# A two-layer backbone kernel: a new order for the end of the first projection

## The chip, the cores and the metric

The kernel runs on one core of one Trainium2 chip, as a single program. The metric is the device time of one execution in microseconds (us). The core has five engines that run side by side, each through its own instructions in order: TensorE (PE in the profile; its weight loads are PEld), VectorE (DVE), ScalarE (ACT), GpSimd (POOL), and SyncE (SP), which here only issues transfers. Transfers (DMA) are issued from SyncE's or ScalarE's queue, and an issue that has to wait holds up everything behind it on that queue.

## The reference, cut to what matters

Two layers run over 1024 latent tokens and 256 context tokens, 1024 features wide. The change lies in the first layer, windowed attention with 16 query heads in 4 groups, one key and value head per group:

```python
q, k, v, g = jnp.split(h @ w_in, [A_WIDTH, A_WIDTH + A_KV_WIDTH, A_WIDTH + 2 * A_KV_WIDTH], axis=-1)
...
qx = apply_rope(qx, cos, sin)
kx = apply_rope(kx, cos, sin)
...
yx = (ox * jax.nn.silu(gx)) @ w_out
```

`h` is the normalized input, scaled and shifted by a vector that comes from the conditioning (adaLN). `w_in` is 1024 x 2560: columns 0 to 1023 are queries, 1024 to 1279 keys, 1280 to 1535 values, 1536 to 2559 gates. A query block of 128 latent tokens sees its own and the two neighbouring blocks of keys under a band mask, and all context keys; a context block sees the context only. Rope turns queries and keys of latent tokens, not of context tokens. Layer two (latent attention) follows on the result.

## The kernel before, in words

**Arithmetic.** Products that matter are done as three: each factor is split in a rounded high part (a cast on ScalarE, L121) and a low part (a subtraction, L122, on VectorE or GpSimd), and `mm3` (L126 to L128) adds high x high, low x high and high x low.

**First projection.** `w_in` is taken in ten blocks of 256 columns, in the order of the list `blocks`; the first is the values' and is done by tokens. For the other nine, `proj_t(bi, gp, c)` computes one tile: block `bi`, token group `gp` (0: the 256 context tokens; 1 and 2: 512 latent tokens each), half `c` of the block's columns. A latent tile has 24 matmuls of 512 columns; a context tile does both halves, 48 matmuls of 256 columns. I write a tile as (bi, gp, c). What follows the matmuls depends on the columns:

- gates (c0 at 1536 or above): Silu on ScalarE into a buffer (L462), then a store to DRAM from SyncE's queue (L465, L467);
- queries and keys of latent tokens: rope, that is a product and a shuffle on VectorE (L489, L490), a product and, for queries, a sum on GpSimd (L491, L493); then, after the next tile's matmuls are written, `rest()`: the split (ScalarE, VectorE), and one tile later the store of the queries (L510);
- queries of context tokens: split and store only (L478, L483).

Weights come by `fetch(bi)`: four loads into three staging buffers, split on ScalarE and GpSimd within the two tiles after the request. There are two weight places, used in turn. The list `order` says which tile follows which; `next_item()` counts tiles and runs what `later` has put off. All of this stands inside a manual schedule, in which each engine's instructions keep the order in which the code writes them; behind it (from L802) the compiler's scheduler may reorder.

**Beside the tiles**, `ada_steps` computes the remaining adaLN vectors on VectorE (L385) from pieces of `ada_w`, summed by two or one small matmuls (L396), some of them stored as gate vectors (L408).

**The end of the projection.** In before the last two blocks are gates (columns 2048 and 2304), and their tiles are interleaved by token group: (8,1,*), (9,1,*), (8,2,*), (9,2,*), (8,0,0), (9,0,0). In that stretch the kernel also requests and splits the output weights `a_w_out` (16 pieces of 128 x 512, L691, through three staging buffers `wstg`, by `wo_load`, the lower part in turn on GpSimd and VectorE) and prepares the attention. A unit is 128 query tokens times one group of four heads (`UnitA`). `prep_q` loads its queries (four transfers, L566), `prep` its gates (L574), `score(h)` multiplies queries with keys for one head (L590, L591, two or four matmuls), takes the maxima under the mask (L597, VectorE, with L599) and the exponents (L600, ScalarE). `T` transposes them (L618), `PV` multiplies with the values (L628), `fin` and `fin2` finish a unit. In before unit 0's four scores stand whole in front of tile (9,0,0). A tile of the psum memory (`PB`, eight banks) is given out in turn: `pss()` for the projection, banks 0 to 2 for scores.

The memory of gates and tables is shared by offset: the mask lies where the cosines lay, the gate vectors `gx` where the sines and, after the change, a staging buffer lie.

Of the kernel before, what the change touches and what calls it, by code (L numbers as in the profile page):

```python
# [59 lines left out]
def kernel(ctx: ExitStack, tc: tile.TileContext, t, out, dbg=None):  # L60
    nc = tc.nc
# [21 lines left out]
    load = nc.sync.dma_start  # L83
# [35 lines left out]
    def split(hi, lo, src, lo_eng=None):  # L119

        nc.scalar.copy(hi, src)  # L121
        (lo_eng or nc.vector).tensor_sub(lo, src, hi.bitcast(F32))  # L122

    def mm3(o, a, b, first, last):
        (ah, al), (bh, bl) = a, b
        nc.tensor.matmul(o, ah, bh, start=first, stop=False)  # L126
        nc.tensor.matmul(o, al, bh, start=False, stop=False)  # L127
        nc.tensor.matmul(o, ah, bl, start=False, stop=last)  # L128
# [135 lines left out]
        return t["x"][(i - 2) * 128 : (i - 1) * 128, :]  # L264

    w_in = t["a_w_in"]
    blocks = [1280, 0, 1536, 256, 1792, 512, 768, 1024, 2048, 2304]
    wt = {}


# [171 lines left out]
        hw.append(two.rearrange("p (q s k n) -> p q s k n", q=2, s=2, k=8))  # L442
    swap = [(i + 16) % 32 for i in range(32)]

    def proj_t(bi, gp, c):
        W, c0 = wt[bi], blocks[bi]
        ps = PB[:, 4, :] if (bi, gp) == (9, 0) else pss()
        for cc in (c,) if gp else range(2):
            if gp:
                o = shp(ps, 2, 256)  # L450
            else:
                o = ps[:, cc * 256 : cc * 256 + 256]
            for k in range(8):
                if gp:
                    m = [hw[gp][:, :, s, k, :] for s in range(2)]
                else:
                    m = [hT[0][:, s, k, :] for s in range(2)]
                mm3(o, [W[:, s, k, cc * 128 : cc * 128 + 128] for s in range(2)], m, k == 0, k == 7)
        t0 = 256 + 512 * (gp - 1) if gp else 0
        if c0 >= 1536:  # L460
            g = ev.next()
            nc.scalar.activation(g, ps, AF.Silu)  # L462
            ch = (c0 - 1536) // 128
            if gp:
                load(out=g0_d[ch + c, :, t0 : t0 + 512], in_=g)  # L465
            else:
                load(out=g0_d[ch : ch + 2, :, 0:256].rearrange("c p n -> p c n"), in_=shp(g, 2, 256))  # L467
            return None
        if gp == 0:
            if c0 == 1024:  # L470
                u = shp(ps, 2, 256)
                for e in range(2):
                    kh = kT[:, e::2, 0:256]
                    split(kh[0:64], kh[64:128], u[64 * e : 64 * e + 64])
            else:
                q = shp(qst.next(), 2, 2, 2, 128)
                u = shp(ps, 2, 2, 128)
                split(q[:, :, :, 0].bitcast(F32R), q[:, :, :, 1].bitcast(F32R), u)  # L478

                def store():  # L480
                    for cc in range(2):
                        dst = q0_d[c0 // 256, cc, :, :, 0:2].rearrange("e p t s n -> (e p) (t s n)")
                        load(out=dst, in_=q[:, cc].rearrange("p t s n -> p (t s n)"))  # L483

                later(1, store)
            return None
        x0 = t0 - 256
        a, r = ev.next(), ev.next()
        nc.vector.tensor_mul(a, ps, cosa[:, x0 : x0 + 512])  # L489
        nc.vector.stream_shuffle(out=r, in_=ps, mask=swap)  # L490
        nc.gpsimd.tensor_mul(r, r, sina[:, x0 : x0 + 512])  # L491
        if c0 < 1024:
            nc.gpsimd.tensor_add(a, a, r)  # L493
# [23 lines left out]
    gx = f_at(8, 1024)  # L517
    gc = f_at(48, 1024)
    ytmp = Ring(F, [12], 512)
    wstg = Ring(F, [4, 6, 12], 512)  # L520
    rbr = Ring(F, [42, 47], 256)
    or1, or2, rtr = (Ring(F, [o, o - 5], 256) for o in (43, 44, 45))
    Pr = Ring(F, [14 + 2.5 * i for i in range(8)], 640)
# [156 lines left out]
    units = [UnitA(ti, g) for ti in ORDER for g in range(4)]  # L680


    def wo_load():
        engs = [nc.gpsimd, nc.vector]
        pieces = [(k, slice(c * 512, c * 512 + 512)) for k in range(8) for c in range(2)]
        staged = []
        for i in range(len(pieces) + 2):
            if i < len(pieces):
                k, cs = pieces[i]
                st = wstg.next()  # L690
                load(out=st, in_=t["a_w_out"][k * 128 : k * 128 + 128, cs])  # L691
                staged.append((k, cs, st))
            if i >= 2:
                k, cs, st = staged.pop(0)
                split(Wo[k][:, 0, cs], Wo[k][:, 1, cs], st, engs[i % 2])
                yield

    wo_fill = wo_load()
    order = [(bi, gp, c) for bi in range(1, 8) for gp in range(3) for c in range(2 if gp else 1)]
    order += [(bi, gp, c) for gp in (1, 2, 0) for bi in (8, 9) for c in range(2 if gp else 1)]  # L700
    rest = None


# [65 lines left out]

    in_order = tc.manual_schedule()  # L770
    in_order.__enter__()
    for bi, gp, c in order:
        next_item()
        if bi + 1 < 10 and bi + 1 not in started:
            started.add(bi + 1)
            fetch(bi + 1)
        steps(ada_steps, 1 if gp and blocks[bi] < 1536 else 2)
        if (bi, gp, c) == (9, 2, 0):
            load2(out=mask, in_=t["mask"])
            load2(out=gx, in_=gate_d[0, 0, :].partition_broadcast(128))  # L780
            load2(out=gc, in_=gate_d[0, 1, :].partition_broadcast(128))
        if (bi, gp) == (8, 0):
            units[0].prep_q()
            units[0].prep()
            units[1].prep_q()
        if (bi, gp) == (9, 0):
            units[1].prep()
            units[2].prep_q()
            for h in range(4):
                units[0].score(h)  # L790
        r = proj_t(bi, gp, c)
        if rest:
            rest()
        rest = r
        if bi >= 8 and gp != 1:
            for _ in range(2):
                next(wo_fill, None)

    while due:
        next_item()  # L800
# [13 lines left out]
    og = None  # L814
    fins = []
    for ui, u in enumerate(units):
        if ui in (1, 2):
            next(wo_fill, None)
            next(wo_fill, None)
        if u.g == 0:  # L820
            og = shp(ogr.next(), 2, 8, 128)
            steps = 4 * u.m - 2
# [737 lines left out]
```

## Time and profile before

| what | value |
|---|---|
| median of 3 runs | 1650.68 us (1650.03 to 1650.99) |
| the profiled execution | 1647.58 us |
| its span, first to last instruction | 1645.8 us |
| mean granted TensorE clock | 0.994 |
| TensorE busy | 1588.9 us, 97% of the span |
| ScalarE, VectorE, GpSimd busy | 825.8, 991.7, 801.4 us |

How to read it: the profile is of one execution; each row is an instruction or a group with its line in the code, `out<-in` by the program's names, and in brackets the idle time before it with what ended it. A `q` behind an engine's name (SPq, ACTq) is its queue, issuing a transfer. The granted clock is the share of full speed that TensorE had. Matmuls are pipelined, so a row's length is more than the distance to the next one, and it is the distance that counts.

### The profile page before, as it was taken

Reading aid. Unit: us, or ns where it says so; the run is one execution under the profiler, and the core shown is the slowest. Engines: PE = TensorE matmul, PEld = TensorE weight load, DVE = VectorE, ACT = ScalarE, POOL = GpSimd, SP = SyncE. Lnnn points to the kernel's source line nnn. Section 1 sums busy time; section 2 is a strip of 40 time slices with the busy share of each in tenths; the row PEclk is TensorE's granted clock in tenths of the full one; section 3 lists DMA queues with packets and bytes.
Section 4 is the critical chain, followed back from the end, with each engine's and each line's share of the span. In section 5 each row is a group of like instructions: output and inputs, shape, how many; then the busy total and the mean of one; then the engine's idle time right before and its main releaser. Section 6 shows DMA issues by size and latency. Waiting matters only on the chain.

```text
span 1645.8 us, 23776 instructions
## 1 busy us (share of the span) xinstructions
PE 1588.9 (97%) x8156; PEld 1211.1 (74%) x8156; DVE 991.7 (60%) x1972; ACT 825.8 (50%) x1779; POOL 801.4 (49%) x776
## 2 busy tenths in 40 slices
PE   7899999988999999998999999999999999999998
PEld 2687888776878888878887887566766756666687
DVE  1786878648888888878444005655455455455354
ACT  3622121249777777777323324555555555555421
POOL 1453456214543333344245422786676777668510
PEclk9999999999999999999999999999999999999999
DMA  8535445374333222235127722211111111122151
GB/s 279 158 116 192 165 162 173 117 220 138 98 107 93 92 90 90 91 109 176 52 78 249 231 67 87 77 52 36 39 39 36 45 37 38 46 80 70 47 160 64
DMA packets 122467, 176.75 MB, mean 107 GB/s; under 512 B 11485, under 2 KB 71517, under 8 KB 122345
## 3 DMA queue, kind: packets, MB, share of 16 engines
q1 hardware_dynamic: 120184, 171.12, 32.7%
q10 hardware_dynamic: 2160, 4.11, 0.8%
q8 instruction: 64, 1.05, 0.3%
q14 instruction: 59, 0.48, 0.1%
HBM read 129.04 MB, written 46.15 MB: 106 GB/s over the span
## 4 chain that ended last, share of the span: by engine, by line
PE 75%; DVE 8%; ACT 6%; issue 5%; POOL 3%; DMA 2%; SPq 0%; ACTq 0%; DVEq 0%; POOLq 0%
PE PB L126 17%; PE PB L128 16%; PE PB L127 16%; PE PB L1233 9%; PE PB L1199 4%; PE PB L628 3%; PE PB L618 3%; DVE arena_r L122 2%; PE PB L590 2%; PE PB L591 1%; DVE arena_f L597 1%; ACT arena_r L121 1%; ACT arena_f L600 1%; DVE arena_f L202 1%; ACT arena_f L1218 1%
## 5 line engine op out<-in xcount | busy, mean ns | idle before, releaser
L126 PE MATMUL PB<-arena_r 128*128 128x512 f32 (+3 forms) x1632 | 605.6, 372 | 6.3 <-ACT arena_r L205 3.8
L127 PE MATMUL PB<-arena_r 128*128 128x512 f32 (+3 forms) x1632 | 597.4, 366 | 5.1 <-DVE arena_r L207 3.9
L128 PE MATMUL PB<-arena_r 128*128 128x512 f32 (+3 forms) x1632 | 594.5, 366 | 0.2 <-DVE arena_r L122 0.2
L126 PEld LDWEIGHTS PB<-arena_r 128*128 128x128 f32 (+1 forms) x1632 | 309.2, 190 | 96.3 <-issue 32.0
L1225 POOL TENSOR_TENSOR arena_f<-arena_f 128x512 f32<-128x512 f32 x252 | 327.5, 1299 | 75.4 <-ACT arena_f L1218 60.1
L128 PEld LDWEIGHTS PB<-arena_r 128*128 128x128 f32 (+1 forms) x1632 | 309.2, 190 | 49.9 <-issue 1.2
L127 PEld LDWEIGHTS PB<-arena_r 128*128 128x128 f32 (+1 forms) x1632 | 310.4, 190 | 47.8 <-DVE arena_r L207 5.1
L1203 DVE TENSOR_REDUCE arena_f<-PB 128x1 f32<-128x1280 f32 x128 | 190.4, 1488 | 104.9 <-PE PB L1199 102.4
L1218 ACT ACTIVATE arena_f<-PB 128x512 f32<-128x512 f32 x320 | 189.1, 598 | 124.7 <-PE PB L128 111.8
L122 DVE TENSOR_TENSOR arena_r<-PB,arena_r 128x512 fp32r<-128x512 f32 (+4 forms) x255 | 162.5, 644 | 120.7 <-ACT arena_r L121 118.8
L122 POOL TENSOR_TENSOR arena_r<-arena_f,arena_r 128x512 fp32r<-128x512 f32 x84 | 116.7, 1402 | 192.3 <-ACT arena_r L121 165.2
L121 ACT CAST arena_r<-PB 128x512 fp32r<-128x512 f32 (+4 forms) x255 | 138.2, 549 | 67.6 <-PE PB L618 30.7
L597 DVE CUSTOM_DVE_ANT_0 arena_f<-PB,arena_f,small 128x256 f32<-128x256 f32 (+1 forms) x288 | 145.5, 522 | 26.9 <-PE PB L591 20.2
L1233 PE MATMUL PB<-arena_f 128*64 128x512 f32 x640 | 157.1, 600 | 0.0
L600 ACT ACTIVATE arena_f<-arena_f,small 128x640 f32<-128x640 f32 (+2 forms) x160 | 119.3, 746 | 32.7 <-DVE small L599 32.2
L628 PE MATMUL PB<-arena_r 128*128 128x512 f32 x336 | 123.5, 441 | 4.0 <-ACT arena_f L639 2.5
L385 DVE SCALAR_TENSOR_TENSOR arena_f<-arena_f,small 128x512 f32<-128x512 f32 x98 | 114.1, 1208 | 11.4 <-DMA arena_f<-ada_w 11.0
L618 PE MATMUL PB<-ident,arena_f 128*128 128x128 f32 x672 | 111.3, 274 | 2.2 <-ACT arena_f L600 1.2
L121 ACT CAST arena_r<-arena_f 128x512 fp32r<-128x512 f32 (+1 forms) x124 | 72.9, 608 | 75.8 <-DMA arena_f<-a_w_in 21.2
L1233 PEld LDWEIGHTS PB<-arena_f 128*64 128x64 f32 x640 | 43.5, 136 | 80.9 <-issue 79.4
L1199 PE MATMUL PB<-arena_r 96*128 96x512 f32 (+1 forms) x384 | 99.8, 367 | 0.3 <-DVE arena_f L1203 0.2
L618 PEld LDWEIGHTS PB<-ident,arena_f 128*128 128x128 f32 x672 | 83.5, 140 | 20.9 <-ACT arena_f L600 5.4
(151 smaller groups left out, 1788.8 us busy)
## 6 DMA issues: line engine op xcount, KB each, us to landing
arena_r<-q_d SPq DMA_DIRECT2D x160, 128.0 KB, 2.9
arena_f<-ada_w SPq DMA_DIRECT2D x68, 256.0 KB, 3.1
arena_f<-a_w_in SPq DMA_DIRECT2D x40, 256.0 KB, 3.7
arena_f<-x SPq DMA_DIRECT2D x16, 512.0 KB, 3.9
q_d<-arena_f SPq DMA_DIRECT2D x16, 512.0 KB, 2.6
qn_d<-arena_f SPq DMA_DIRECT2D x16, 512.0 KB, 4.5
arena_r<-qn_d SPq DMA_DIRECT2D x32, 256.0 KB, 3.6
arena_f<-ada_w SPq DMA_DIRECT2D x14, 512.0 KB, 6.0
```

Source lines behind the costliest of these rows:

```text
L121: nc.scalar.copy(hi, src)
L122: (lo_eng or nc.vector).tensor_sub(lo, src, hi.bitcast(F32))
L126: nc.tensor.matmul(o, ah, bh, start=first, stop=False)
L127: nc.tensor.matmul(o, al, bh, start=False, stop=False)
L128: nc.tensor.matmul(o, ah, bl, start=False, stop=last)
L618: nc.tensor.transpose(pt[:, h, :], self.Ps[h][:, ci * 128 : ci * 128 + 128], ident)
L628: nc.tensor.matmul(self.pv, V[:, self.chunks[ci], self.g, :], PT[:, s], start=ci == 0 and s == 0, stop=ci == self.m - 1 and s == 1,)
L1199: nc.tensor.matmul(psm[:, n0 : n0 + n], self.qT[0:96, 0, b * 128 : b * 128 + 128], kt[0:96, 0, n0 : n0 + n], start=True, stop=True,)
L1203: nc.vector.reduce_max(self.mx[:, 96 + b : 97 + b], psm[:, 0:TOK], AX.X, negate=True)
L1218: nc.scalar.activation(E, S, AF.Exp)
L1225: eng.tensor_add(self.acc, self.acc, E)
L1233: nc.tensor.matmul(self.pv[p : p + 64], Vq[:, c, self.h % 4, :], self.E.pop(c), start=c < 2, stop=c >= NT - 2)
```

## The change

Six edits, all around the end of the first projection:

1. `blocks`: the order of the last blocks becomes gates 2048, keys 1024, gates 2304, queries 768 (it was queries 768, keys 1024, gates 2048, gates 2304).
2. `order`: the last two blocks run (8,1,*), (8,2,*), (9,1,*), (9,2,*), then (8,0,0) and (9,0,0).
3. Gate stores go out on ScalarE's queue (`load2`) instead of SyncE's (`load`).
4. Output weights: `wo_get(3)` requests three pieces after each of the last five tiles, `wo_cut(3)` splits three before that after each of the last four (GpSimd, VectorE, GpSimd); the rest follows at units 0 and 1 on GpSimd. The third staging buffer moves from 12 to 8.
5. `proj_t` takes a list of functions and runs one after every fourth step of its inner loop, so unit 0's four scores stand inside tile (9,0,0), behind its 6th, 18th, 30th and 42nd matmul.
6. The mask is loaded at tile (8,0,0) instead of (9,2,0), the gate vectors `gx` and `gc` at unit 2 instead of (9,2,0).

```diff
-    blocks = [1280, 0, 1536, 256, 1792, 512, 768, 1024, 2048, 2304]
+    blocks = [1280, 0, 1536, 256, 1792, 512, 2048, 1024, 2304, 768]
...
-    def proj_t(bi, gp, c):
+    def proj_t(bi, gp, c, between=()):
+        between = iter(between)
...
                 mm3(o, [W[:, s, k, cc * 128 : cc * 128 + 128] for s in range(2)], m, k == 0, k == 7)
+                if k % 4 == 1:
+                    for fn in [next(between, None)]:
+                        fn and fn()
...
-                load(out=g0_d[ch + c, :, t0 : t0 + 512], in_=g)
+                load2(out=g0_d[ch + c, :, t0 : t0 + 512], in_=g)
             else:
-                load(out=g0_d[ch : ch + 2, :, 0:256].rearrange("c p n -> p c n"), in_=shp(g, 2, 256))
+                load2(out=g0_d[ch : ch + 2, :, 0:256].rearrange("c p n -> p c n"), in_=shp(g, 2, 256))
...
-    wstg = Ring(F, [4, 6, 12], 512)
+    wstg = Ring(F, [4, 6, 8], 512)
...
+    def wo_get(n):
+        for _ in range(min(n, len(wo_pieces))):
+            k, cs = wo_pieces.pop(0)
+            wo_got.append((k, cs, wstg.next()))
+            load(out=wo_got[-1][2], in_=t["a_w_out"][k * 128 : k * 128 + 128, cs])
+
+    def wo_cut(n, engs):
+        for i in range(min(n, len(wo_got))):
+            k, cs, st = wo_got.pop(0)
+            split(Wo[k][:, 0, cs], Wo[k][:, 1, cs], st, engs[i % len(engs)])
...
-    order += [(bi, gp, c) for gp in (1, 2, 0) for bi in (8, 9) for c in range(2 if gp else 1)]
+    order += [(bi, gp, c) for bi in (8, 9) for gp in (1, 2) for c in range(2)] + [(8, 0, 0), (9, 0, 0)]
+    tail = len(order) - 5
...
-        steps(ada_steps, 1 if gp and blocks[bi] < 1536 else 2)
-        if (bi, gp, c) == (9, 2, 0):
-            load2(out=mask, in_=t["mask"])
-            load2(out=gx, in_=gate_d[0, 0, :].partition_broadcast(128))
-            load2(out=gc, in_=gate_d[0, 1, :].partition_broadcast(128))
         if (bi, gp) == (8, 0):
             units[0].prep_q()
+            load2(out=mask, in_=t["mask"])
             units[0].prep()
             units[1].prep_q()
         if (bi, gp) == (9, 0):
             units[1].prep()
             units[2].prep_q()
-            for h in range(4):
-                units[0].score(h)
-        r = proj_t(bi, gp, c)
+            first = [lambda h=h: units[0].score(h) for h in range(4)]
+        steps(ada_steps, 1 if gp and blocks[bi] < 1536 else 2)
+        r = proj_t(bi, gp, c, first if (bi, gp) == (9, 0) else ())
         if rest:
             rest()
         rest = r
-        if bi >= 8 and gp != 1:
-            for _ in range(2):
-                next(wo_fill, None)
+        if at > tail:
+            wo_cut(3, [nc.gpsimd, nc.vector, nc.gpsimd])
+        if at >= tail:
+            wo_get(3)
...
-        if ui in (1, 2):
-            next(wo_fill, None)
-            next(wo_fill, None)
+        if ui < 2:
+            wo_cut(3, [nc.gpsimd])
+            wo_get(3)
+        if ui == 2:
+            load2(out=gx, in_=gate_d[0, 0, :].partition_broadcast(128))
+            load2(out=gc, in_=gate_d[0, 1, :].partition_broadcast(128))
```

More of the change, by code (lines that the diff above doesn't have):

```diff
@@ L680 @@
     units = [UnitA(ti, g) for ti in ORDER for g in range(4)]
[L683 to L698, printed above, removed]
+    wo_pieces = [(k, slice(c * 512, c * 512 + 512)) for k in range(8) for c in range(2)]
+    wo_got = []
+    def wo_get(n):
[7 more added lines that the diff above has]
+            split(Wo[k][:, 0, cs], Wo[k][:, 1, cs], st, engs[i % len(engs)])
     order = [(bi, gp, c) for bi in range(1, 8) for gp in range(3) for c in range(2 if gp else 1)]
-    order += [(bi, gp, c) for gp in (1, 2, 0) for bi in (8, 9) for c in range(2 if gp else 1)]
+    order += [(bi, gp, c) for bi in (8, 9) for gp in (1, 2) for c in range(2)] + [(8, 0, 0), (9, 0, 0)]
+    tail = len(order) - 5
     rest = None
@@ L771 @@
     in_order.__enter__()
-    for bi, gp, c in order:
+    for at, (bi, gp, c) in enumerate(order):
         next_item()
```

## The prediction

> **What bounds the kernel now.** I read the page's first line, then the surroundings of the change in the table of stretches (us from the span's start; length; busy time and instructions of PE, PEld, DVE, ACT, POOL; granted clock; DMA share; GB/s).
>
> ```profile
> span 1645.8 us, 23776 instructions
> ```
>
> ```profile
> 300.00:346.50 46.50, 43.68 (x184) 33.17 (x183) 22.31 (x26) 11.74 (x20) 9.86 (x8) 1.00 0.57 183
> 346.50:365.60 19.10, 16.55 (x114) 15.28 (x113) 7.58 (x26) 8.10 (x16) 2.56 (x2) 0.91 0.73 203
> 357.00:361.00 4.00, 3.91 (x18) 3.56 (x18) 3.02 (x16) 2.77 (x7) 0.00 (x0) 0.57 0.91 266
> 365.60:400.00 34.40, 30.57 (x190) 24.52 (x189) 30.91 (x115) 32.98 (x82) 13.94 (x18) 1.00 0.49 142
> ```
>
> TensorE is the bound: up to 346.5 it is busy for all but 2.8 us, so only its holes can be won. Then it does the two context tiles (8,0,0) and (9,0,0) until 365.6 and, between them, four scores; after 365.6 ScalarE is busy for 32.98 of 34.40 us and is the engine to watch. The holes, from TensorE's timeline:
>
> ```profile
> 312.59 0.51 PE L126 MATMUL PB<-arena_r 128*128 128x512 f32 x1 [0.33 <-ACT arena_r L121]
> 313.93 0.50 PE L127 MATMUL PB<-arena_r 128*128 128x512 f32 x1 [0.84 <-POOL arena_r L122]
> ...
> 339.93 0.59 PE L396 MATMUL PB<-arena_f,small 128*1 128x512 f32 x1 [1.60 <-DVE arena_f L385]
> ...
> 346.27 0.39 PE L128 MATMUL PB<-arena_r 128*128 128x512 f32 x1
> 346.49 0.28 PE L126 MATMUL PB<-arena_r 128*128 128x256 f32 x1
> ...
> 352.13 0.28 PE L128 MATMUL PB<-arena_r 128*128 128x256 f32 x1
> 354.54 0.36 PE L590 MATMUL PB<-arena_r 128*128 128x256 f32 x1 [2.14 <-DMA arena_r<-q_d]
> ...
> 365.49 0.28 PE L590 MATMUL PB<-arena_r 128*128 128x256 f32 x1
> ```
>
> Three holes: 1.17 us at 312-314 (last quarter of block 9's weights), 1.60 us at 339.9 (an adaLN sum), and the scores. From 346.49 to 352.13 lie 48 matmuls of (8,0,0), one per 0.12 us; a 512-wide one takes 0.22 (346.27 to 346.49). The scores' first matmul waits for the queries' load until 354.54. From 352.25 to 365.49, 13.2 us, TensorE does 16 score matmuls and the 48 of (9,0,0), worth 64 x 0.12 = 7.7: 5.5 us are lost there. 1.7 of them are the clock: 0.57 over 357-361 means 0.43 / 0.5 x 4 = 3.4 us at half speed. SyncE's queue, and what it waited for from 300 to 420, tell why the queries are late:
>
> ```profile
> SPq L465 <- ACT arena_f L462: 23.7, 6, 4.9
> SPq L691 <- POOL arena_r L122: 10.0, 5, 3.7
> ```
>
> ```profile
> 347.78 2.19 SPq L691 DMA_DIRECT2D arena_f<-a_w_out  x2
> 350.02 0.28 SPq L408 DMA_DIRECT2D gate_d<-arena_f  x1
> 350.40 0.69 SPq L566 DMA_DIRECT2D arena_r<-q_d  x1
> ```
>
> SyncE stood behind gate stores and output-weight loads. Unit 0's queries are asked for at 350.40 and used 4.14 us later.
>
> **The change, part by part** (times on the clock of before).
>
> *Gate stores to ScalarE's queue.* SyncE loses waits of 23.7 us; ScalarE gains an issue per store. Cost 0 before 365: ScalarE is busy for 11.74 of 46.5 and 8.10 of 19.1 us. Were that cover gone, each would cost the 0.34 to 0.48 of its present issues (rows below).
> The Trainium skill, page "DMA: Bandwidth & Descriptors", section "Issuing engines are not separate DMA queues", speaks against it: another issuing engine saves only the issue time, as all share 16 DMA engines. The trace differs in that the wait, not the issue, held SyncE; by page or row the sum gets 0, for no hole of TensorE names a gate store.
>
> *Order of the last blocks.* Block 9's weights, asked for at block 8's start, are now first used four tiles later instead of two: the 1.17 us goes. The adaLN sum's products no longer sit behind output-weight requests, and one more gate block ahead of block 8 moves them earlier: the 1.60 us goes. Sum -2.8, so the last 512-wide tile, (9,2,1), ends at 343.7 instead of 346.5. Bounds -2 (a new short wait) and -3.3.
>
> *Queries as last block.* This is the expensive part: rope now runs on GpSimd in the very tiles in which it should cut output weights. In before the last ten tiles are all gates, and GpSimd is idle there. A query tile of before, VectorE, then GpSimd, then a cut among rope work:
>
> ```profile
> 226.40 0.69 DVE L489 TENSOR_TENSOR arena_f<-PB,arena_f 128x512 f32<-128x512 f32 x1 [1.76 <-PE PB L128]
> ```
>
> ```profile
> 225.75 1.29 POOL L122 TENSOR_TENSOR arena_r<-arena_f,arena_r 128x512 fp32r<-128x512 f32 x1
> 227.83 1.64 POOL L491 TENSOR_TENSOR arena_f<-arena_f 128x512 f32<-128x512 f32 x1 [0.79 <-DVE arena_f L490]
> 229.55 1.62 POOL L493 TENSOR_TENSOR arena_f<-arena_f 128x512 f32<-128x512 f32 x1
> ...
> 244.73 1.55 POOL L122 TENSOR_TENSOR arena_r<-arena_f,arena_r 128x512 fp32r<-128x512 f32 x1 [2.68 <-ACT arena_r L121]
> ```
>
> GpSimd's rope ends 229.55 + 1.62 - 226.40 = 4.8 us after the tile's psum is read, about 4.9 after the tile's end; a cut costs it 1.29 (up to 1.55).
>
> *Output weights a tile early.* Sixteen pieces pass three buffers, three per tile; two of three are cut on GpSimd, each cut stands behind the rope of its own tile, and the next three requests wait on SyncE for the cuts. Durations of loads of the weights, then of the queries, to landing:
>
> ```profile
> DMA to landing us min/median/max: 2.6/3.0/3.4
> ```
>
> ```profile
> DMA to landing us min/median/max: 2.6/2.9/5.0
> ```
>
> The chain: (9,2,0) ends at 343.7 - 24 x 0.225 = 338.3, its rope at 343.2; two cuts of the first three pieces, 345.8; rope of (9,2,1), ready 0.15 + 1.43 after 343.7, starts at 345.8, ends at 349.1; the second three, last one requested at 345.9 and landed at 348.9, cut on GpSimd until 349.1 + 2 x 1.29 = 351.7. Only then does SyncE issue the last of the third three (0.4), a query store (0.4), and from 352.5 unit 0's queries: first score at 352.5 + 4.14 = **356.7**. It is the early request itself that delays the queries: they stand behind it on SyncE, and with them unit 1's queries and gates, not needed until 365.
>
> *First scores inside the last tile.* TensorE ends (8,0,0) at 343.7 + 5.76 = 349.5, does six matmuls of (9,0,0) and stands at the first score from 350.2 to 356.7: 6.5 us with 42 matmuls of the tile behind it. Then 16 + 42 = 58 x 0.12 = 7.0 us, plus half clock. I take the stretch seen, 1.7 us lost (bounds 0, as until 357, and 3.4, two such stretches). VectorE's maxima and the exponents go beside the tile, so their pace no longer counts. End: **365.4**, against 365.49: -0.1.
> The Trainium skill, "TensorE: Matmul & The Clock Gate", section "What's actually happening", gives half speed after an idle window of about 3.4 us and full speed after about 3.4 us busy. Before shows it already after a 2.1 us hole with sparse scores behind; by the page a hole of 6.5 us has it too, so the end is 365.4 by either.
> The mask's load, now behind the second cuts on ScalarE's queue (349.4), may take up to 7 us before it is the later one; its landing isn't shown.
>
> *Behind the tile*, ScalarE:
>
> ```profile
> L121 ACT CAST arena_r<-arena_f 128x512 fp32r<-128x512 f32 x6 | 3.5, 622 | 0.0
> ...
> L462 ACT ACT_TABLE_LOAD x1 | 1.3, 1283 | 4.4 <-PE PB L128 4.4
> L600 ACT ACT_TABLE_LOAD x1 | 1.3, 1283 | 0.0
> ...
> L462 ACT ACTIVATE arena_f<-PB 128x512 f32<-128x512 f32 x1 | 0.6, 598 | 0.0
> ```
>
> ```profile
> 337.31 0.48 ACTq L780 DMA_DIRECT2D arena_f<-gate_d  x1
> ...
> 360.43 0.72 ACT L600 ACTIVATE arena_f<-arena_f,small 128x512 f32<-128x512 f32 x1 [0.41 <-DVE small L599]
> 361.06 0.19 ACT L600 ACTIVATION_READ_ACCUMULATOR arena_f<-arena_f,small 128x1 f32 x1
> ```
>
> Gone behind 365.6: two table loads and a Silu, 3.2 us. New there: the last head's exponent, 0.9; the query cast, 0.6; a seventh weight cast, 0.6; two gate-vector issues at unit 2, 1.0: 3.1 us. Sum -0.1; as to order, bounds -2 and +1. VectorE is even (one cut and a query subtraction for three cuts).
>
> Sum: -0.1 - 0.1 = -0.2, and the profiled span 1645.6. The median of the runs before, 1650.68, lies 3.1 above the profiled execution's 1647.58, so the difference is carried over: **1650.5 us**. With the bounds of its terms this case runs from 1647.5 to 1654.
>
> **The rivals.**
> *Faster: the queries arrive in time.* If GpSimd cut the weights ahead of its rope, SyncE would reach the queries before 346, and only the mask would make TensorE wait, about 1 us. End: 349.5 + 7.7 + 1 = 358.2, 7.3 earlier: 1643.4 us. For it: SyncE loses 23.7 us of waits. Against: POOL's rows run one after another in the order written, and 244.73 shows cuts behind rope. Chance 0.18.
> *Slower: the same wait, longer.* Place: the first score inside (9,0,0). Each us by which the queries land after 356.7 is a us of the kernel; a landing of 5.0 for 2.9 (+2.1), four cuts at 1.55 (+1.0), and a second stretch at half clock (+1.7) give +4.8: 1655.5 us. It decides from a first score after 360.0. For it: everything up to that score is one chain without slack. Against: 5.0 is the longest landing seen. Chance 0.22.
> The same page says that the gate's window runs freely, which by itself allows that second stretch; no run here shows its phase.
> *Slightly faster: ScalarE's relief carries on.* The table loads go at once, the gate vectors and seventh cast come later, perhaps into slack: -2.5, 1648.2. For it: ScalarE is idle for only 1.4 of 34.4 us after 365.6. Against: unit 0's last exponent now lies there too. Chance 0.14.
> That the change does not do what it says is the forecast: its holes close and one opens.
>
> **How the numbers follow.** Forecast 0.46. About 0.2% (3.3 us) is what a measurement of this kernel can tell from no change. Faster by more: 0.18 and a third of the last rival, 0.23. Slower by more: 0.22. Within: 0.55. The range 1644.5 to 1655.5 leaves out most of the faster rival and a little of the slower one, and holds the bounds of the forecast's terms.
>
> **What would show it.** Right: no hole at 312 or at the adaLN sum; cuts on GpSimd straight behind rope; SyncE asking for unit 0's queries about 8.8 us after (9,2,1) ends; a hole of 5 to 8 us at the first score, inside (9,0,0), released by the queries' load; clock under 1 behind it; units' scores at about the same time as now. Wrong: the first score without a wait (the faster rival), a hole at another line, or a different end with the same hole.

## The result, and the profile after

| | before | after |
|---|---|---|
| median of 12 runs | 1649.97 us | 1651.15 us |
| lowest and highest | 1645.31, 1651.34 | 1649.69, 1652.85 |
| profiled execution, its span | 1647.58, 1645.8 | 1652.48, 1650.3 |
| mean granted clock | 0.994 | 0.990 |

The ratio is 1.0013, with a 95% interval of 1.0004 to 1.0022: 2.1 us slower (0.7 to 3.6; a ratio's distance from 1, times 1650); the two medians lie 1.2 us apart. I had forecast 0.2 us faster. That the median of 1651.15 lies only 0.65 above the 1650.5 of the forecast is in part luck: its baseline, 1650.68 from three runs, is 1649.97 with twelve.

In the diff's region all line numbers are 4 higher after the change: L594 and L595 are the scores, L570 the queries' loads, L694 the output weights' loads, L514 the queries' stores, L495 and L497 GpSimd's rope. First the table of stretches of after (columns as in the prediction; first column from and to, last three granted clock, DMA share, GB/s).

```profile
300.00:343.80 43.80, 42.10 (x180) 32.88 (x180) 21.90 (x31) 9.64 (x17) 15.25 (x11) 1.00 0.32 108
343.80:350.25 6.45, 6.45 (x55) 6.41 (x53) 3.42 (x5) 1.97 (x4) 6.32 (x5) 1.00 0.63 200
350.25:359.21 8.96, 0.22 (x2) 0.04 (x2) 1.88 (x3) 4.35 (x7) 3.96 (x3) 0.73 0.95 283
359.21:364.50 5.29, 5.29 (x25) 5.29 (x26) 2.06 (x9) 0.81 (x2) 0.00 (x0) 0.50 0.97 267
364.50:368.65 4.15, 4.15 (x36) 4.15 (x35) 1.97 (x11) 1.63 (x4) 0.00 (x0) 0.98 0.97 278
```

The hole at 312 is gone, and the one at the scores has grown: TensorE does next to nothing from 350.25 to 359.21, while the DMA engines are busy for 0.95 of the time, and then works for 5.29 us at half clock (to 364.50, where I cut the stretch). TensorE's timeline has the same hole:

```profile
303.49 1.02 PE L396 MATMUL PB<-arena_f,small 128*1 128x512 f32 x2 [1.70 <-DVE arena_f L385]
...
343.84 0.28 PE L126 MATMUL PB<-arena_r 128*128 128x256 f32 x1
...
350.19 0.28 PE L128 MATMUL PB<-arena_r 128*128 128x256 f32 x1
359.21 0.55 PE L594 MATMUL PB<-arena_r 128*128 128x256 f32 x1 [8.75 <-DMA arena_r<-q_d]
...
368.65 0.28 PE L594 MATMUL PB<-arena_r 128*128 128x256 f32 x1
```

The last row is unit 1's first score, that is the end of tile (9,0,0): 368.65, where before had 365.49. The first row is the adaLN sum's wait, which has moved from 339.9 to 303.5 and not gone. GpSimd and SyncE, which the forecast had as one chain, in after:

```profile
340.09 1.57 POOL L495 TENSOR_TENSOR arena_f<-arena_f 128x512 f32<-128x512 f32 x1 [3.62 <-DVE arena_f L494]
341.74 1.62 POOL L497 TENSOR_TENSOR arena_f<-arena_f 128x512 f32<-128x512 f32 x1
343.32 2.54 POOL L122 TENSOR_TENSOR arena_r<-arena_f,arena_r 128x512 fp32r<-128x512 f32 x2
345.82 1.74 POOL L495 TENSOR_TENSOR arena_f<-arena_f 128x512 f32<-128x512 f32 x1
...
350.43 1.44 POOL L122 TENSOR_TENSOR arena_r<-arena_f,arena_r 128x512 fp32r<-128x512 f32 x1 [0.23 <-ACT arena_r L121]
```

```profile
350.23 2.00 SPq L694 DMA_DIRECT2D arena_f<-a_w_out  x3
352.27 0.49 SPq L514 DMA_DIRECT2D q_d<-arena_f  x1
352.86 3.23 SPq L570 DMA_DIRECT2D arena_r<-q_d  x4
```

Rope, two cuts, rope, two cuts, and only then three weight loads' issues, a store and unit 0's queries: asked for at 352.86, used at 359.21, 6.35 us later. The landing times (the loads of the weights, then of the queries) show the difference to before, whose longest were 3.4 and 5.0:

```profile
DMA to landing us min/median/max: 2.6/3.5/5.9
```

```profile
DMA to landing us min/median/max: 2.6/2.9/6.8
```

**How traces are compared here.** Up to the start of tile (2,0,0), the first gate tile, the kernels have the same work, and yet it starts between 116.59 and 119.44 us in the fourteen traces of this study. So I count from there. The rows of before, then after:

```profile
119.02 0.28 PE L126 MATMUL PB<-arena_r 128*128 128x256 f32 x1
```

```profile
118.56 0.28 PE L126 MATMUL PB<-arena_r 128*128 128x256 f32 x1
```

By this count the last product with the values, the end of the attention, is 4.2 us later in after than in before (735.2 - 118.56 against 731.4 - 119.02), while the ratio gives 2.1. Before's one profiled execution is 2.4 us shorter than its median, and the change's is 1.3 longer than its own; trace differences *to before* come out some 2 us too high for the kernels below. In which stretch before's execution was the shorter one, no run shows. Differences to the change agree with the ratios to 1.6 us for all twelve kernels below.

### The profile page after: what moved, and what is told of

The parts are those of the page before. It is cut to its first block, busy times and chain, and to the rows that moved or that the text cites. A ratio compares the mean times of both kernels' runs of the same rounds, so it can differ in the third digit from the quotient of the medians.

```text
span 1650.3 us, 23755 instructions
## 1 busy us (share of the span) xinstructions
PE 1589.7 (96%) x8156; PEld 1213.8 (74%) x8156; DVE 981.4 (59%) x1968; ACT 823.1 (50%) x1777; POOL 803.2 (49%) x780
## 4 chain that ended last, share of the span: by engine, by line
PE 75%; DVE 9%; ACT 5%; issue 5%; POOL 3%; DMA 2%; SPq 0%; DVEq 0%; POOLq 0%; ACTq 0%
PE PB L126 17%; PE PB L128 16%; PE PB L127 16%; PE PB L1236 9%; PE PB L1202 4%; PE PB L632 4%; PE PB L622 3%; PE PB L594 2%; DVE arena_r L122 2%; PE PB L595 2%; DVE arena_f L601 1%; DVE arena_f L385 1%; ACT arena_f L604 1%; POOL arena_r L122 1%; PE PB L1261 1%
## 5 line engine op out<-in xcount | busy, mean ns | idle before, releaser
L122 POOL TENSOR_TENSOR arena_r<-arena_f,arena_r 128x512 fp32r<-128x512 f32 x88 | 120.8, 1388 | 178.6 <-ACT arena_r L121 159.0
L601 DVE CUSTOM_DVE_ANT_0 arena_f<-PB,arena_f,small 128x256 f32<-128x256 f32 (+1 forms) x288 | 145.7, 523 | 34.0 <-PE PB L595 27.0
L385 DVE SCALAR_TENSOR_TENSOR arena_f<-arena_f,small 128x512 f32<-128x512 f32 x98 | 104.1, 1110 | 5.9 <-DMA arena_f<-ada_w 5.6
L594 PE MATMUL PB<-arena_r 128*128 128x256 f32 (+1 forms) x288 | 87.4, 320 | 12.3 <-DMA arena_r<-q_d 8.7
```

What stands on the lines that cost most here:

```text
L601: nc.vector.tensor_tensor_reduce(o, S, mk, 1.0, prev, ALU.add, ALU.max, mx)
```

## The experiments

All are compared with before; 5 to 11 runs each. In us: the ratio's distance from 1 times 1650; then, counted from the start of (2,0,0) in each trace, when unit 0's queries are asked for, the first score, the end of tile (9,0,0) (unit 1's first score; in 9 a transpose comes there first and is taken), and the last product with the values.

| kernel | ratio [95%] | us | asked | first score | tile ends | last product |
|---|---|---|---|---|---|---|
| before | 1 | 0 | 231.4 | 235.5 | 246.5 | 612.4 |
| the change | 1.0013 [1.0004, 1.0022] | +2.1 | 234.3 | 240.7 | 250.1 | 616.6 |
| 1 queries first | 0.9987 [0.9978, 0.9996] | -2.1 | 228.5 | 235.1 | 246.0 | 612.1 |
| 2 cuts on VectorE | 1.0010 [1.0001, 1.0018] | +1.7 | 232.8 | 239.5 | 248.4 | 615.6 |
| 3 scores ahead | 1.0017 [1.0008, 1.0026] | +2.8 | 234.3 | 240.8 | 251.0 | 617.2 |
| 4 gate stores alone | 0.9978 [0.9969, 0.9987] | -3.6 | 229.6 | 234.3 | 244.9 | 611.1 |
| 5 before, three edits | 0.9965 [0.9951, 0.9978] | -5.8 | 222.3 | 231.9 | 240.2 | 608.5 |
| 6 third three small | 0.9995 [0.9986, 1.0003] | -0.8 | 234.3 | 239.4 | 248.1 | 613.5 |
| 7 array kept busy | 1.0007 [0.9998, 1.0016] | +1.2 | 234.3 | 241.5 | 248.5 | 614.6 |
| 8 gates last | 1.0006 [0.9997, 1.0015] | +1.0 | 231.6 | 236.9 | 246.5 | 616.5 |
| 9 queries first, GpSimd cuts | 0.9987 [0.9979, 0.9996] | -2.1 | 228.5 | 234.4 | 242.9 | 611.2 |
| 10 gate stores back | 1.0008 [0.9999, 1.0016] | +1.3 | 234.2 | 241.4 | 250.8 | 617.3 |
| 11 two edits, scores ahead | 0.9978 [0.9969, 0.9987] | -3.6 | 222.9 | 232.5 | 245.8 | 611.5 |
| 12 three edits, GpSimd cuts | 0.9947 [0.9934, 0.9961] | -8.7 | 222.4 | 232.1 | 239.1 | 605.2 |

My theory was the forecast's: the first score waits for queries that stand on SyncE behind weight requests, which wait for GpSimd's cuts behind its rope. The rivals: the queries' landing in a crowd of transfers; the clock; and that a part I held to be free (the gate stores) is not. Differences between two kernels below are differences of their ratios, unless a trace is named.

**1. The change, queries first.**

```diff
         if (bi, gp) == (8, 0):
-            units[0].prep_q()
...
         rest = r
+        if (bi, gp, c) == (9, 2, 1):
+            units[0].prep_q()
         if at > tail:
             wo_cut(3, [nc.gpsimd, nc.vector, nc.gpsimd])
```

> The changed kernel, but unit 0's queries are asked for at the end of tile (9,2,1), ahead of the cut and request of the third three pieces of output weights, instead of at tile (8,0,0) behind them. Theory (SyncE's order holds the queries up): SyncE reaches them at about 347 instead of 352.9, they land by 351 to 352, the hole of 8.7 us at the first score shrinks to 1 to 3 us (then the mask, asked for at 349.7, is last), and the kernel is 6 to 9 us faster than the change, 4 to 7 us faster than before. Rival (the queries are slow because the 16 transfer engines are crowded, whoever asks first): they still land about 6 us after their issue, near 353, and the mask near 355; 3 to 5 us faster than the change. Rival (scores inside the tile cost by themselves): no more than 1 us.

Measured: 4.2 us faster than the change, less than the 6 to 9 of the theory and within the 3 to 5 of the crowd's rival. The queries leave 5.8 us earlier, so the order on SyncE did hold them. But the first score still comes 6.65 us after the request, and behind it stands a new wait, on TensorE and VectorE:

```profile
353.35 0.36 PE L594 MATMUL PB<-arena_r 128*128 128x256 f32 x1 [3.20 <-DMA arena_r<-q_d]
...
357.91 0.58 PE L594 MATMUL PB<-arena_r 128*128 128x256 f32 x1 [1.17 <-DVE small L601]
```

```profile
356.23 1.23 DVE L122 TENSOR_TENSOR arena_r<-arena_f,arena_r 128x512 fp32r<-128x512 f32 x1 [3.62 <-ACT arena_r L121]
357.38 0.47 DVE L601 CUSTOM_DVE_ANT_0 arena_f<-PB,arena_f,small 128x256 f32<-128x256 f32 x1
```

A weight cut stands in front of unit 0's first maxima (L601) and itself waits for a weight load. The first score's wait was hiding this one.

**2. The change, cuts of the last tiles on VectorE.**

```diff
-            wo_cut(3, [nc.gpsimd, nc.vector, nc.gpsimd])
+            wo_cut(3, [nc.vector])
```

> The changed kernel, but within the last four tiles all pieces of output weights are cut on VectorE, none on GpSimd behind rope. Theory (cuts behind rope on GpSimd hold SyncE): the third three pieces are asked for by 349 instead of 352, the queries' first issue comes at 349.5 to 350.5 instead of 352.9, the first score at 354 to 356 instead of 359.2: 3 to 5 us faster than the change. Rival (it is the landing of the requested pieces, not GpSimd, that sets the pace): under 1.5 us.

Measured: 0.4 us faster than the change, which can't be told from zero, and not 3 to 5. Taking the cuts off GpSimd moves the request by only 1.5 us, and the first score by 1.1. The first three cuts on VectorE, durations in ns (min/median/max):

```profile
L122 DVE TENSOR_TENSOR arena_r<-arena_f,arena_r x3: 679/1776/1782, 340.1 to 343.5; 128x512 fp32r<-128x512 f32 x3
```

The two beside GpSimd's rope take 1.78 us each, more than the 1.3 of a cut on GpSimd in the change; only the third, behind rope's end, takes 0.68.

**3. The change, scores ahead of the tile.**

```diff
-            first = [lambda h=h: units[0].score(h) for h in range(4)]
...
-        r = proj_t(bi, gp, c, first if (bi, gp) == (9, 0) else ())
+            for h in range(4):
+                units[0].score(h)
...
+        r = proj_t(bi, gp, c)
```

> The changed kernel, but unit 0's four scores stand whole in front of tile (9,0,0), as before. Theory: the same hole, 0.6 us longer at its start, and then the scores at VectorE's pace of 1.2 us per head in front of the tile: the tile ends 1 to 2.5 us later than in the change. Rival (the wait inside the tile is what costs, as it holds up 42 matmuls): the tile ends earlier than in the change.

Measured: the tile ends 0.9 us later than in the change (1 to 2.5 were expected), the kernel 0.7 (the intervals overlap). Where the queries are late, scores inside the tile are worth under 1 us.

**4. Before, with the gate stores alone.**

```diff
-                load(out=g0_d[ch + c, :, t0 : t0 + 512], in_=g)
+                load2(out=g0_d[ch + c, :, t0 : t0 + 512], in_=g)
```

and the same for the context tile's store.

> The kernel before, with the gate stores on ScalarE's queue and nothing else. Theory: SyncE's waits for Silu (23.7 us) go, but the queries still stand behind the output weights, whose request waits for a cut on GpSimd until 349.6; within 0.5 us of before. Rival (the gate stores held up the queries and the adaLN pieces): the 1.6 us hole at 339.9 and part of the 2.1 us hole go, 2 to 3 us faster than before.

Measured: 3.6 us faster than before (2.1 to 5.1). My theory, nothing, fell. SyncE in before, then SyncE and TensorE in this kernel:

```profile
328.18 0.33 SPq L465 DMA_DIRECT2D g_d<-arena_f  x1
328.60 6.02 SPq L691 DMA_DIRECT2D arena_f<-a_w_out  x4
334.71 0.86 SPq L364 DMA_DIRECT2D arena_f<-ada_w  x2
```

```profile
328.66 0.86 SPq L364 DMA_DIRECT2D arena_f<-ada_w  x2
```

```profile
312.99 1.02 PE L396 MATMUL PB<-arena_f,small 128*1 128x512 f32 x2
335.93 1.02 PE L396 MATMUL PB<-arena_f,small 128*1 128x512 f32 x2
```

The adaLN sums (L396) have lost their 1.60 us wait. The last pieces of `ada_w` for the sum come over SyncE; in before they leave at 334.71, behind weight requests that wait for a cut, and these stood behind a gate store that waited until 328.18. Counted from (2,0,0) they leave 3.9 us earlier here. No hole named a gate store, because what the hole named stood two steps behind it. The queries leave 1.8 us earlier too, and the tile ends 1.6 us earlier.

**5. Before, with three edits**: gate stores as in 4, unit 0's queries at the end of (9,2,1) ahead of the last weight pieces, as in 1, and the scores inside (9,0,0) as in the change; block order and weight requests as before.

> The kernel before with three edits: gate stores on ScalarE's queue (measured alone: 3.6 us faster), unit 0's queries asked for ahead of the last two pieces of output weights, and unit 0's scores inside tile (9,0,0). Blocks, order and output weights stay as before. Theory (SyncE's order sets the first score, and the scores' pace hides inside the tile): queries asked for at 343, landed by 348.5, no hole of more than 1.5 us; (9,0,0) ends at 357 instead of 361.6: 3.5 to 5 us faster than the gate stores alone, 7 to 9 us faster than before. Rival (crowded transfers): the queries land 6 us and more after their issue, and the gain over the gate stores alone is 1.5 to 3 us.

Measured: 5.8 us faster than before (3.6 to 8.1; 7 to 9 were expected). Asked for 9.1 us earlier than before, the queries are there when TensorE comes to the first score. One wait is left in the tile, 1.00 us, and again it is for the maxima (L601) behind a cut on VectorE.

**6. The change, with the third three weight pieces small** (64 of 512 columns).

```diff
-            load(out=wo_got[-1][2], in_=t["a_w_out"][k * 128 : k * 128 + 128, cs])
+            c0 = cs.start
+            load(out=wo_got[-1][2][:, 0:cols], in_=t["a_w_out"][k * 128 : k * 128 + 128, c0 : c0 + cols])
...
-            wo_get(3)
+            wo_get(3, 64 if at == tail + 2 else 512)
```

> The changed kernel, but of the third three pieces of output weights, the ones that stand right in front of the queries on SyncE's queue, only one eighth (64 of 512 columns) is loaded; the rest of the buffer is left as it was, so part of the computation works on other weights. Waits and order stay. Theory (the queries land late because these pieces move at the same time): from the queries' first issue to the first score 4 to 4.8 us instead of 6.35, the hole 1.5 to 2.5 us shorter, the kernel 1.5 to 2.5 us faster than the change. Rival (the landing is slow for another reason, such as the query store in front of it or the mask): under 0.7 us.

It isolates these three loads, as the request stays where it was (234.3). From the queries' first issue to the first score in three kernels (before, this one, the change):

```profile
350.40:354.54 4.14, 2.00 (x17) 1.83 (x17) 0.38 (x1) 2.02 (x4) 0.86 (x1) 1.00 0.62 182
```

```profile
350.91:356.03 5.12, 0.00 (x1) 0.03 (x1) 1.46 (x2) 2.77 (x4) 2.65 (x2) 0.69 0.80 249
```

```profile
352.86:359.21 6.35, 0.00 (x0) 0.03 (x1) 0.69 (x1) 3.13 (x4) 2.52 (x2) 0.63 1.00 318
```

With the DMA engines 0.62, 0.80 and 1.00 busy it takes 4.14, 5.12 and 6.35 us. Making the three loads small gives back 1.2 of the extra 2.2 us (4 to 4.8 us were expected for the 5.12), and the kernel runs 2.9 us faster than the change (3.1 by the last product; 2.0 at the tile's end). At 0.9995 [0.9986, 1.0003] it is back where the forecast had the change.

By the code of `prep_q` and `score(0)`, the first score reads the first and the third of the four transfers (in 1, the third lands 4.7 us after its issue at 348.50, just before the first score at 353.35). The third's issue in before and in the change:

```profile
351.82 0.60 SPq L566 DMA_DIRECT2D arena_r<-q_d  x1
```

```profile
354.81 0.63 SPq L570 DMA_DIRECT2D arena_r<-q_d  x1
```

It comes 1.42 us behind the first issue in before and 1.95 in the change, so 0.5 of the 2.2 us is slower issuing; from the third's issue to the first score it is 2.72 us in before and 4.40 in the change, so 1.7 is landing. Experiment 6 has 1.42 and 3.70: the small loads take back the whole of the issuing and 0.7 of the landing. Which transfers make up the other 1.0 was not taken apart.

**7. The change, with TensorE kept busy**: 70 matmuls into an idle bank ahead of the first score.

```diff
+            def spin():
+                for _ in range(70):
+                    nc.tensor.matmul(PB[:, 7, 0:256], wt[9][:, 0, 0, 0:128], hT[0][:, 0, 0, :], start=True, stop=True)
+                units[0].score(0)
+
+            first[0] = spin
```

> The changed kernel with 70 more matmuls of 256 columns, into an unused bank, in front of the first score, 8.4 us of work in a hole of 8.7. Theory (the hole costs its length and the half clock behind it): the clock stays at 1.00, the 58 matmuls behind the first score take 7.0 us instead of 9.9, the kernel is 2 to 3 us faster than the change although it does more. Rival (the clock costs nothing here, as other engines set the pace behind the hole): within 0.7 us of the change.

```profile
360.24:364.50 4.26, 4.26 (x35) 4.26 (x36) 2.27 (x10) 1.29 (x3) 0.00 (x0) 1.00 0.86 220
364.50:367.27 2.77, 2.77 (x25) 2.77 (x24) 1.75 (x8) 1.16 (x4) 0.00 (x0) 1.00 1.01 360
```

The first score is 0.8 us later than in the change (241.5 against 240.7), and yet the tile ends 1.6 earlier: its 58 matmuls take 7.03 us at clock 1.00, against 9.44 in the change (359.21 to 368.65). So 2.4 us of the change's tile are the clock. The kernel moved by 1.0 us, with overlapping intervals, between the 2 to 3 of the theory and the 0.7 of the rival.

**8. The change, with before's list of blocks**, so that the last two blocks are gates again.

```diff
-    blocks = [1280, 0, 1536, 256, 1792, 512, 2048, 1024, 2304, 768]
+    blocks = [1280, 0, 1536, 256, 1792, 512, 768, 1024, 2048, 2304]
```

> The changed kernel with the list of blocks of before (the last two blocks are gates again, the other five edits stay). Theory (rope on GpSimd in front of the cuts holds the output weights and so the queries): no rope and no query store near the end, the third three pieces asked for by 349, the queries' first issue at 349 to 350, the first score at 354 to 356: 3 to 5 us faster than the change. Rival (the two table loads and the Silu behind the tile, which come back, cost as much as the hole gives): within 1 us of the change.

Measured: without rope GpSimd cuts at once, the queries leave 2.7 us earlier and the tile ends 3.6 us earlier. But a Silu and two table loads come back on ScalarE right behind the tile:

```profile
365.22 1.28 ACT L466 ACT_TABLE_LOAD   x1
366.51 0.60 ACT L466 ACTIVATE arena_f<-PB 128x512 f32<-128x512 f32 x1
367.13 1.28 ACT L604 ACT_TABLE_LOAD   x1
```

By the last product all but 0.1 of the 3.6 us is gone, and the kernel is only 1.1 us faster than the change (intervals overlap). So queries as last block do relieve ScalarE, as the rival "ScalarE's relief" had it, and cost about as much through GpSimd's rope. That the two table loads and the Silu eat the 3.6 us is read from their 3.2 us in these rows; no run takes them out alone.

**9. The change, queries first, three cuts behind (8,0,0) on GpSimd.** As 1, and

```diff
-            wo_cut(3, [nc.gpsimd, nc.vector, nc.gpsimd])
+            wo_cut(3, [nc.gpsimd] if (bi, gp) == (8, 0) else [nc.gpsimd, nc.vector, nc.gpsimd])
```

> The change with unit 0's queries asked for at the end of tile (9,2,1), ahead of the weight cuts and requests, and with the three cuts behind tile (8,0,0) all on GpSimd, so that VectorE has no cut in front of unit 0's first maxima. My theory (of what remained when the queries alone went first, the 1.17 us hole at the second score is VectorE's cut): first score at about 353, no hole behind the scores over 0.3 us, about 1.2 us less than with the queries first alone, so some 1645 us. Rival (the hole only moves: the half clock behind the first score and the later cuts on GpSimd take it back): within 0.5 us of the queries first alone, 1646.2.

Measured: the wait on the maxima is gone and the tile ends 3.1 us earlier than in 1, but the kernel is no faster (both 0.9987). The last product is 0.8 earlier, so over 2 us are given back in the attention, as the rival had it. Most of it goes early: in 9 TensorE waits 1.72 us at 375.04 for a subtraction on VectorE, where 1 has a wait of 0.51 at that place (378.83).

**10. The change, gate stores back on SyncE's queue** (edit 3 of the change undone).

> The change with its gate stores back on SyncE's queue, all else as in the change. Alone, in the kernel before, moving them gave -3.6 us. My theory (that gain was SyncE reaching unit 0's queries early, which in the change the weights' cuts behind GpSimd's rope prevent anyway; what is left is the adaLN holes): the first score at the same distance from the start of tile (8,0,0) as in the change, 15.4 us, within 0.5; one or two more short holes before it; kernel 0 to 2 us slower than the change. Rival (the two gains add): 3 to 4 us slower than the change, about 1654.5, with the first score later by that much.

Measured: 0.8 us faster than the change by the ratios, 0.7 later by the last product: nothing that can be told from zero. Tile (8,0,0) starts 225.29 us after (2,0,0), in the change 225.28 (343.84 - 118.56), so no new hole opened before it; the first score is 16.1 us behind that start, 0.7 more than in the change (0.5 at most was expected). The gains do not add. I read it so: what the stores give alone, the change's block order takes anyway, and its weights hold SyncE afterwards.

**11. Before, gate stores and early queries, scores ahead of the tile** (5 without its third edit).

> The kernel before with its gate stores on ScalarE's queue and unit 0's queries asked for at the end of tile (9,2,1), ahead of the last weight pieces; the scores stand whole in front of tile (9,0,0) as before. It splits the version that also puts them inside the tile (1643.1 us). My theory (in time, the queries need no tile around the scores; the maxima on VectorE then pace them, and a tile around them hides that): first score without a wait on the queries, some 2 to 3 us of short holes on VectorE's maxima between the scores, 1 to 2 us slower than with the scores inside: 1644 to 1645. Rival (queries early are the whole gain): equal within 0.5 us, 1643.

Measured: 0.9978, the same as gate stores alone, though the queries leave 6.7 us earlier. VectorE, then TensorE:

```profile
353.50 1.34 DVE L122 TENSOR_TENSOR arena_r<-arena_f,arena_r 128x512 fp32r<-128x512 f32 x1 [3.70 <-ACT arena_r L121]
```

```profile
355.30 0.58 PE L594 MATMUL PB<-arena_r 128*128 128x256 f32 x1 [2.41 <-DVE small L601]
```

The cut in front of the maxima makes TensorE wait 2.41 us, and half clock sets in during the wait (0.50 from 354.00 to 360.82). With the queries in time, the scores inside the tile are worth 5.6 us at its end (245.8 against 240.2) and 2.2 us by the ratios (1 to 2 were expected; the intervals overlap).

**12. The three edits of 5, with all weight cuts on GpSimd.**

```diff
-        engs = [nc.gpsimd, nc.vector]
+        engs = [nc.gpsimd]
...
-                split(Wo[k][:, 0, cs], Wo[k][:, 1, cs], st, engs[i % 2])
+                split(Wo[k][:, 0, cs], Wo[k][:, 1, cs], st, engs[0])
```

> The kernel before with three edits (gate stores on ScalarE's queue, unit 0's queries asked for at the end of tile (9,2,1), scores inside tile (9,0,0)), measured at 1643.1 us, and now all cuts of the output weights on GpSimd instead of in turn with VectorE. In the version with turns one cut of 1.36 us on VectorE stands in front of unit 0's first maxima and TensorE waits 1.00 us for them. My theory: that wait goes and the tile ends about 1 us earlier counted from the start of tile (2,0,0), 239.2 instead of 240.2, but the gain is given back behind the tile, where ScalarE is the bound: the kernel within 1 us of 1643.1. Rival (the whole microsecond stays): 1642 or less, with the last product with the values earlier by the same 1 us.

Measured: 1640.72 us, 8.7 us faster than before (6.4 to 10.9), the fastest of all. The tile ends at 239.1 as expected, with no wait in it, but here the gain stays and grows: the last product is 3.3 us earlier than in 5. The rival was right. The interval overlaps that of 5 (3.6 to 8.1), so how much the cuts alone are worth stays open.

## Why the prediction was wrong

The forecast's picture held in the main: the hole at 312 closed, the adaLN wait only moved, a large hole opened at the first score inside (9,0,0), and its row names the queries' load. Its sum of -0.2 failed in four terms, here against the trace.

- **"Sum -2.8"** for the order of the last blocks. Tile (8,0,0) starts 2.19 us earlier, from 227.47 (346.49 - 119.02) to 225.28. The adaLN wait only moved, 1.70 us at 303.5 for 1.60 at 339.9; that the sum still came out near is luck: the weights' hole, with the small gaps around it, was worth about 2.3 us (2.19 + 0.10) and not 1.17. Error 0.6.
- **"from 352.5 unit 0's queries"**, 8.8 us after (9,2,1) ends: 9.02 measured (352.86 - 343.84). The hardest part of the forecast, a chain over four engines, was right to 0.2.
- **"first score at 352.5 + 4.14"**. This is the step that failed: 6.35, so 2.2 more. I took the time of a moment at which the DMA engines were 0.62 busy, while my own chain put three fresh weight loads directly ahead of the queries. Experiment 6 shows that these loads make up 1.2 of the 2.2; the other 1.0 stays open. The price stood in the slower rival, which I had as a chance of a long landing (+2.1); it was a consequence of the change.
- **"I take the stretch seen, 1.7 us lost"** for half clock: 58 matmuls took 9.44 us for 7.0, so 2.4 lost (as by experiment 7). Error 0.7, within its bounds.

Together 0.6 + 0.2 + 2.2 + 0.7 = 3.7 us at the tile's end, and there the trace has +3.6 (250.09 against 246.47) for a forecast of -0.1. Behind the tile, -0.1 forecast: from the tile's end to the last product before takes 365.9 us and after 366.6, so +0.6; why was not tested. That makes 4.2 by the traces and 2.1 by the ratio; the difference goes with the two profiled executions, told above.

**The gate stores.** "No hole of TensorE names a gate store" was a wrong reason for a term that came out right by luck. Within the change the stores are worth nothing measurable (10); in the kernel before they are worth 3.6 us (4). Rows of waits on SyncE said 23.7 us; I asked which hole names the store, and should have asked what was queued behind it: the `ada_w` pieces and the queries. The rule that I weighed (the Trainium skill, "DMA: Bandwidth & Descriptors", "Issuing engines are not separate DMA queues": another issuer saves only the issue) does not cover this case: experiment 4 changes the issuer alone and gains 3.6 us, and its rows show what stood behind the wait at the queue's head leaving 3.9 us earlier.

**The rivals.** *Slower, the same wait longer* had the right mechanism; its threshold, a first score after 360.0, was just missed (359.21, or 359.67 on before's clock, 0.46 later at (2,0,0)), and its price of +4.8 was not reached. *Faster, the queries in time* had the queries reached before 346, in which case the tile would end 7.3 us earlier. In the change itself, with the queries asked for at 346.70 (1) and 345.95 (9), it ends only 0.5 and 3.6 us earlier than in before, as the queries still take some 6 us to the first score. Experiment 12 ends it 7.3 us earlier (239.1 against 246.5), but with before's block order; that the figures agree is chance. *ScalarE's relief* seems to exist (8), but is paid for by rope.

## What to carry to other kernels

Price a wait at the head of a transfer queue by what stands behind it, two steps on, and not by which hole names it. Take a landing time from a moment as crowded as the one that the change will make, and where a change hands loads to the queue ahead of the needed one, raise it. When a wait is removed, look at the next engine in line: here queries in time uncovered a weight cut in front of the maxima (1, 5, 11), and the largest gain measured came with both gone (12).

## What the runs showed of the hardware

- **Issuing slows too.** The four issues of the queries take 2.67 us in before and 3.23 in the change; one of them took 1.11 for 0.60. With the small loads of 6 they take 2.67.
- **A cut on VectorE doubles beside GpSimd.** In experiment 9, on VectorE:

```profile
348.13 1.54 DVE L122 TENSOR_TENSOR arena_r<-arena_f,arena_r 128x512 fp32r<-128x512 f32 x1 [2.80 <-ACT arena_r L121]
350.92 0.69 DVE L122 TENSOR_TENSOR arena_f<-arena_f 128x512 fp32r<-128x512 f32 x1 [1.24 <-ACT arena_f L121]
```

```profile
347.82 2.97 POOL L122 TENSOR_TENSOR arena_r<-arena_f,arena_r 128x512 fp32r<-128x512 f32 x2
```

  The second block is GpSimd's: it is at work during VectorE's first row and idle during the second. The Trainium skill, "SBUF — State Buffer", section "SBUF: two separate sides", says that an operation of VectorE with two inputs there and one of GpSimd that reads there exclude each other, the later one waiting for the whole of the earlier. The rows fit: 0.69 for the work leaves 0.85 of waiting, to 348.98, and GpSimd's first of two (1.31 us) ends at 349.13; its second takes 1.72. That would explain why moving cuts to VectorE brought little (2) and moving them off it more (12), but no run separates it from the order of the cuts.
- **Half clock lasts longer than I took.** In the rows below it comes in stretches of about 3.4 us or a multiple. The granted clock (the number after the busy times) in the change, then in before and in 1:

```profile
350.50:354.45 3.95, 0.00 (x0) 0.00 (x0) 0.94 (x2) 1.50 (x3) 1.37 (x1) 1.00 0.90 250
354.46:364.69 10.23, 5.47 (x26) 5.51 (x26) 2.90 (x11) 3.41 (x6) 2.52 (x2) 0.50 1.00 294
364.70:374.93 10.23, 9.03 (x68) 8.18 (x68) 8.01 (x33) 7.07 (x17) 2.97 (x2) 1.00 0.56 160
374.94:378.34 3.40, 3.40 (x13) 2.74 (x12) 2.93 (x12) 3.09 (x8) 2.43 (x2) 0.50 0.87 286
```

```profile
357.27:360.67 3.40, 3.40 (x14) 3.13 (x15) 2.90 (x14) 2.17 (x7) 0.00 (x0) 0.50 0.91 262
```

```profile
354.33:361.14 6.81, 5.64 (x27) 5.35 (x26) 3.32 (x11) 4.64 (x8) 2.56 (x2) 0.50 0.90 284
```

  The stretches are 10.2, 3.4 and 6.8 us long. In the change the half clock sets in 4 us into the hole, and 5.5 us of it lie behind the first score. The Trainium skill, "TensorE: Matmul & The Clock Gate", "What's actually happening", which the prediction cites, gives a window of about 3.4 us that runs freely and full speed after about one such window of work. The lengths of the stretches agree with the window; the 5.5 us of work at half clock are more than one. A second stretch follows in the change at 374.94, behind the tile, where before has none; what it costs was not measured. With a hole of 1.17 us left, there was no half clock up to 400 us (7).
- **The preparation varies.** The same code reaches tile (2,0,0) at 116.59 to 119.44 us, as much as the effects measured here.
